# A 3x3 convolution on one core: two images on the partitions in place of two halves of one, inputs resident, and a different first and last stage

## The chip, the core and the metric

The kernel runs on one NeuronCore of a Trainium2 chip. The metric is the device time of one execution in microseconds (us). A second view is one profiled execution, whose span runs from the first to the last instruction.

## What is computed

A batch of 16 images of 64 channels, 64 by 64, is convolved with 128 filters of 64 x 3 x 3, with a border of zeros. A tenth of the weights is non-zero, but the kernels here treat them as dense.

```python
x:      (16, 64, 64, 64) float32
weight: (128, 64, 3, 3)  float32, about 90% zeros
x_pad = np.pad(x, ((0, 0), (0, 0), (1, 1), (1, 1)))
for b, co, ci, kh, kw:
    output[b, co] += weight[co, ci, kh, kw] * x_pad[b, ci, kh:kh+64, kw:kw+64]
output: (16, 128, 64, 64) float32
```

## The kernel before

For each of the nine taps (kh, kw), TensorE multiplies the tap's 64 x 128 weights by the input rows, shifted by the tap, and adds up in PSUM. One tap has only 64 input channels, so it fills half of the 128 rows of the array. The kernel therefore uses both halves at once: of each image, the upper 33 rows lie on partitions 0 to 63 and the lower 33 rows on partitions 64 to 127. One matmul for the upper half and one for the lower half stand next to each other in the program and run side by side. The 33rd row is read twice, since both halves need the rows at the seam.

A unit of work is 8 output rows of each half: two PSUM tiles (of 8, one bank each), nine pairs of matmuls of up to 512 columns (L175), then two copies from PSUM to the float32 output image in SBUF. An image has four units; the last unit of image 15 is split in two of 4 rows.

**Start.** The weights come in one transfer on SP's queue (L64), are cast to bf16 by VectorE in three pieces (L70), and are transposed on TensorE against an identity matrix (L84): nine taps, once for each half of the partitions, 18 small matmuls, copied out by ScalarE (L91). The identity is built on GpSimd (`make_identity`). Image 0 is loaded in four transfers, the first ten rows of each half first (L54 to L59). All loads of x are issued by GpSimd and cast float32 to bf16 on the way.

**Middle.** Images 1 to 14 are loaded in pairs into three buffers `xsg` (L107, L111), so from the fourth pair on a load waits until a buffer has been used up. Copies from PSUM alternate between ScalarE and VectorE (L186). Images 0, 1 and 12 leave in one transfer each (L202), images 2 to 11 in transfers of two images (L204), all on SP's queue.

**End.** Images 13, 14 and 15 are streamed: after each unit, both its blocks leave in one transfer, by turns on SP's queue (L197) and ScalarE's (L199).

The order of instructions on each engine is that of the program, as the tile framework schedules it; it sets waits where a buffer is reused.

Of the kernel before, what the change touches and what calls it, by code (L numbers as in the profile page):

```python
# [1 line left out]

# [6 lines left out]
FP32 = mybir.dt.float32  # L10
BF16 = mybir.dt.bfloat16


POS_ORDER = [(1, 1), (1, 0), (1, 2), (0, 0), (0, 1), (0, 2), (2, 0), (2, 1), (2, 2)]
CHUNK_ORDER = [1, 0, 2]


@with_exitstack
def kernel(
# [6 lines left out]
    nc = tc.nc  # L26

    B, C_IN, H, W = x.shape
    C_OUT, C_IN2, KH, KW = weight.shape
    assert (C_IN, H, W) == (64, 64, 64) and (C_OUT, KH, KW) == (128, 3, 3)  # L30

    HALF = H // 2
    XROWS = HALF + 1
    SPLIT = 10

    SINGLE_OUT = {0, 1, 12}
    PAIR_OUT_START = {2, 4, 6, 8, 10}
    STREAM_OUT = {13, 14, 15}
    UNITS_8 = [(r, 8) for r in range(0, HALF, 8)]
    STREAM_UNITS = {  # L40
        13: UNITS_8,
        14: UNITS_8,
        15: [(0, 8), (8, 8), (16, 8), (24, 4), (28, 4)],
    }

    const_pool = ctx.enter_context(tc.tile_pool(name="const", bufs=1))
    x0_pool = ctx.enter_context(tc.tile_pool(name="x0", bufs=2))
    xg_pool = ctx.enter_context(tc.tile_pool(name="xg", bufs=3))
    outs_pool = ctx.enter_context(tc.tile_pool(name="osb", bufs=3))
    outg_pool = ctx.enter_context(tc.tile_pool(name="osbg", bufs=2))  # L50
    psum_pool = ctx.enter_context(tc.tile_pool(name="psum", bufs=8, space=bass.MemoryType.PSUM))

    xs0 = x0_pool.tile([128, XROWS, W], BF16, name="xs0")
    nc.gpsimd.dma_start(out=xs0[0:64, 0:SPLIT], in_=x[0, :, 0:SPLIT, :])  # L54
    nc.gpsimd.dma_start(  # L55
        out=xs0[64:128, 0:SPLIT], in_=x[0, :, H - XROWS : H - XROWS + SPLIT, :]
    )
    nc.gpsimd.dma_start(out=xs0[0:64, SPLIT:XROWS], in_=x[0, :, SPLIT:XROWS, :])  # L58
    nc.gpsimd.dma_start(  # L59
        out=xs0[64:128, SPLIT:XROWS], in_=x[0, :, H - XROWS + SPLIT : H, :]  # L60
    )

    w_sb = const_pool.tile([C_OUT, C_IN * KH * KW], FP32)
    nc.sync.dma_start(out=w_sb, in_=weight.rearrange("o i kh kw -> o (i kh kw)"))  # L64
    w_sb3 = w_sb.rearrange("o (i k) -> o i k", k=KH * KW)

    w_bf = const_pool.tile([C_OUT, C_IN * KH * KW], BF16)
    w_bf3 = w_bf.rearrange("o (i k) -> o i k", k=KH * KW)
    for kh in CHUNK_ORDER:
        nc.vector.tensor_copy(  # L70
            out=w_bf3[:, :, kh * KW : (kh + 1) * KW],
            in_=w_sb3[:, :, kh * KW : (kh + 1) * KW],
        )

    ident = const_pool.tile([128, 128], BF16)
    make_identity(nc, ident)

    wT = const_pool.tile([128, KH * KW, C_OUT], BF16)
    for kh in CHUNK_ORDER:
        wps = psum_pool.tile([128, 4, 128], FP32, name="psum_t")  # L80
        for j in range(KW):
            sl = w_bf3[:, :, kh * KW + j]
            for half in range(2):
                nc.tensor.matmul(  # L84
                    wps[half * 64 : (half + 1) * 64, j, :],
                    sl,
                    ident,
                    start=True,
                    stop=True,
                )  # L90
        nc.scalar.copy(out=wT[:, kh * KW : kh * KW + KW, :], in_=wps[:, 0:KW, :])  # L91

    xs_group = None
    oimg_pair = None

    for b in range(B):
        if b == 0:
            xs = xs0
            xsel = ()
        elif b == B - 1:  # L100
            xs = x0_pool.tile([128, XROWS, W], BF16, name="xs15")
            nc.gpsimd.dma_start(out=xs[0:64], in_=x[b, :, 0:XROWS, :])  # L102
            nc.gpsimd.dma_start(out=xs[64:128], in_=x[b, :, H - XROWS : H, :])  # L103
            xsel = ()
        elif b % 2 == 1:
            xs_group = xg_pool.tile([128, 2, XROWS, W], BF16, name="xsg")
            nc.gpsimd.dma_start(  # L107
                out=xs_group[0:64].rearrange("i n r c -> i n (r c)"),
                in_=x[b : b + 2, :, 0:XROWS, :].rearrange("n i r c -> i n (r c)"),
            )  # L110
            nc.gpsimd.dma_start(  # L111
                out=xs_group[64:128].rearrange("i n r c -> i n (r c)"),
                in_=x[b : b + 2, :, H - XROWS : H, :].rearrange(
                    "n i r c -> i n (r c)"
                ),
            )
            xs = xs_group
            xsel = (0,)
        else:
            xs = xs_group  # L120
            xsel = (1,)

        if b in SINGLE_OUT or b in STREAM_OUT:
            oimg = outs_pool.tile([C_OUT, H, W], FP32, name="oimg")
        elif b in PAIR_OUT_START:
            oimg_pair = outg_pool.tile([C_OUT, 2, H, W], FP32, name="oimg2")
            oimg = oimg_pair[:, 0]
        else:
            oimg = oimg_pair[:, 1]

        streamed = b in STREAM_OUT
        if streamed:
            oimg_blk = oimg.rearrange("o (blk r) c -> o blk r c", blk=2)
            out_blk = out[b].rearrange("o (blk r) c -> o blk r c", blk=2)
            units = STREAM_UNITS[b]
        else:
            units = UNITS_8

        for ui, (ur0, rb) in enumerate(units):
            psums = []  # L140
            infos = []
            for half in range(2):
                r0 = half * HALF + ur0
                r1 = r0 + rb
                start_row = 0 if half == 0 else H - XROWS
                pbase = half * 64
                psum_t = psum_pool.tile([128, rb, W], FP32, name="psum_t")
                psums.append(psum_t)
                infos.append((r0, r1, start_row, pbase))

            for idx, (kh, kw) in enumerate(POS_ORDER):
                di, dj = kh - 1, kw - 1
                for half in range(2):
                    r0, r1, start_row, pbase = infos[half]
                    psum_t = psums[half]

                    i_lo = max(r0, -di)
                    i_hi = min(r1, H - di)
                    j_lo = max(0, -dj)
                    j_hi = min(W, W - dj)  # L160

                    rel_lo, rel_hi = i_lo - r0, i_hi - r0
                    xr_lo = i_lo + di - start_row
                    xr_hi = i_hi + di - start_row
                    xc_lo, xc_hi = j_lo + dj, j_hi + dj

                    idx_rhs = (slice(pbase, pbase + 64),) + xsel + (
                        slice(xr_lo, xr_hi),
                        slice(xc_lo, xc_hi),
                    )  # L170
                    rhs = xs[idx_rhs]
                    out_ap = psum_t[:, rel_lo:rel_hi, j_lo:j_hi]
                    lhsT = wT[pbase : pbase + 64, kh * KW + kw, :]

                    nc.tensor.matmul(  # L175
                        out_ap,
                        lhsT,
                        rhs,
                        start=(idx == 0),
                        stop=(idx == len(POS_ORDER) - 1),  # L180
                    )

            if not streamed:
                for half in range(2):
                    r0, r1, _, _ = infos[half]
                    nc.any.tensor_copy(out=oimg[:, r0:r1, :], in_=psums[half])  # L186
            else:
                nc.vector.tensor_copy(  # L188
                    out=oimg[:, infos[0][0] : infos[0][1], :], in_=psums[0]
                )  # L190
                nc.scalar.copy(  # L191
                    out=oimg[:, infos[1][0] : infos[1][1], :], in_=psums[1]
                )
                src = oimg_blk[:, :, ur0 : ur0 + rb, :]
                dst = out_blk[:, :, ur0 : ur0 + rb, :]
                if ui % 2 == 0:
                    nc.sync.dma_start(out=dst, in_=src)  # L197
                else:
                    nc.scalar.dma_start(out=dst, in_=src)  # L199

        if b in SINGLE_OUT:
            nc.sync.dma_start(out=out[b], in_=oimg)  # L202
        elif (b - 1) in PAIR_OUT_START:
            nc.sync.dma_start(  # L204
                out=out[b - 1 : b + 1].rearrange("n o h w -> o n (h w)"),
                in_=oimg_pair.rearrange("o n h w -> o n (h w)"),
            )


# [28 lines left out]
```

## Time and profile before

| what | us |
|---|---|
| median of 3 runs | 137.68 (137.21 to 138.09) |
| span of the profiled execution | 136.1 |
| TensorE busy, in 1188 matmuls | 126.7 |
| weight loads on TensorE, beside them | 77.1 |
| VectorE busy | 45.2 |
| ScalarE busy | 40.2 |
| first product (L175) starts | 5.92 |
| last copy from PSUM starts | 131.54 |

The profiled execution has no time of its own beside its span: what lies around the span is taken from the median, 137.68 - 136.1 = 1.5 us. The DMA engines moved 42.67 MB as they count it (a load that casts is counted by its bf16 bytes); at HBM it is 17.60 MB read and 33.55 MB written.

In the lines of the profile, a group reads: line, engine, operation, what it writes and reads, how often, then busy time and the mean of one in ns. PE is the matmul, PEld the weight load, DVE VectorE, ACT ScalarE, POOL GpSimd, SP SyncE; an engine's name with a q is its queue, here the issue of a DMA. The slices on the page are fortieths of the span.

### The profile page before, as it was taken

The numbers are of one execution on the slowest core, as the hardware profiler recorded it, in microseconds if no ns is written. First come the engines' busy times: TensorE is split into PE (matmuls) and PEld (weight loads), VectorE is DVE, ScalarE is ACT, GpSimd is POOL, SyncE is SP. The second block draws the span as 40 slices with busy tenths as digits, with TensorE's granted clock in tenths as the row PEclk, the third lists the DMA queues.
The fourth block names the chain that finished last, engine by engine and source line by source line (L and its number), as shares of the span: only waits on it lengthen the run. The fifth ranks groups of instructions, "written<-read, shape, count | busy, mean of one in ns | idle before, by whom it ended". The sixth has DMA issues, their size and how long they took to land.

```text
span 136.1 us, 2653 instructions
## 1 busy us (share of the span) xinstructions
PE 126.7 (93%) x1188; PEld 77.1 (57%) x1188; DVE 45.2 (33%) x68; ACT 40.2 (30%) x69; POOL 12.2 (9%) x26
## 2 busy tenths in 40 slices
PE   0699999999999999999999999999999999999960
PEld 0555666666565656665656655665656655656650
DVE  0203432344234432343234423443244333443240
ACT  3302332233323332233223332333233323332230
POOL 6950000003000110003000110000000000000000
PEclk9999999999999999999999999999999999999999
DMA  4999999999999999999999999999509999999884
GB/s 104 119 189 211 216 229 350 363 342 363 245 226 409 443 338 195 302 416 443 274 205 393 438 395 228 294 405 455 231 10 462 385 453 409 389 404 393 329 326 157
DMA packets 7980, 42.67 MB, mean 313 GB/s; under 512 B 673, under 2 KB 1313, under 8 KB 6305
## 3 DMA queue, kind: packets, MB, share of 16 engines
q1 hardware_dynamic: 3840, 30.97, 55.6%
q0 software_dynamic: 2496, 8.65, 33.4%
q10 hardware_dynamic: 1632, 2.88, 5.6%
q8 instruction: 9, 0.15, 0.4%
q14 instruction: 3, 0.02, 0.0%
HBM read 17.60 MB, written 33.55 MB: 376 GB/s over the span
## 4 chain that ended last, share of the span: by engine, by line
PE 92%; POOL 2%; issue 1%; ACT 1%; ACTq 0%; POOLq 0%
PE psum_t L175 91%; PE psum_t L84 1%; ACT oimg L191 1%; POOL xs L54 0%; ACTq L199 0%; POOL xs L55 0%; POOL xsg L107 0%; POOL xs L58 0%; POOL ident masks.py:199 0%; POOL ident masks.py:197 0%; POOL xs L59 0%; POOLq masks.py:199 0%; POOLq L222 0%
## 5 line engine op out<-in xcount | busy, mean ns | idle before, releaser
L175 PE MATMUL psum_t<-xsg,wT 64*128 64x512 bf16 (+2 forms) x1008 | 108.1, 374 | 0.0
L175 PEld LDWEIGHTS <-wT 64*128 64x128 bf16 x1170 | 75.8, 95 | 49.6 <-issue 1.9
L186 DVE COPY oimg<-psum_t 128x512 f32<-128x512 f32 x52 | 36.0, 692 | 68.6 <-PE psum_t L175 68.6
L186 ACT COPY oimg<-psum_t 128x512 f32<-128x512 f32 x52 | 30.5, 586 | 71.7 <-PE psum_t L175 71.7
L175 PE MATMUL psum_t<-xs,wT 64*128 64x504 bf16 (+5 forms) x162 | 18.0, 378 | 0.0
L188 DVE COPY oimg<-psum_t 128x512 f32<-128x512 f32 (+1 forms) x13 | 8.5, 650 | 14.3 <-PE psum_t L175 14.3
L191 ACT COPY oimg<-psum_t 128x512 f32<-128x512 f32 (+1 forms) x13 | 7.2, 554 | 16.0 <-PE psum_t L175 16.0
L107 POOL DMA_DIRECT2D xsg<-in_x_dram x7 | 4.2, 599 | 64.4 <-PE psum_t L175 64.4
L84 PE MATMUL psum_t<-ident,w_bf 128*64 128x128 bf16 x18 | 1.3, 321 | 4.7 <-POOL ident masks.py:199 4.7
L111 POOL DMA_DIRECT2D xsg<-in_x_dram x7 | 4.2, 607 | 0.0
L84 PEld LDWEIGHTS <-w_bf 128*64 128x64 bf16 x18 | 1.3, 208 | 4.5 <-DVE w_bf L70 4.1
L91 ACT CAST wT<-psum_t 128x384 bf16<-128x384 f32 x3 | 1.2, 487 | 3.3 <-PE psum_t L84 3.3
L70 DVE CAST w_bf<-w_sb 128x192 bf16<-128x192 f32 x3 | 0.8, 345 | 3.7 <-DMA w_sb<-in_weight_dram 3.7
L91 ACT ACT_TABLE_LOAD x1 | 1.3, 1283 | 0.7 <-PEq L222 0.7
L54 POOL DMA_DIRECT2D xs<-in_x_dram x1 | 0.7, 659 | 0.8 <-POOLq L222 0.8
L102 POOL DMA_DIRECT2D xs<-in_x_dram x1 | 0.5, 527 | 0.9 <-DMA xs<-in_x_dram 0.9
L103 POOL DMA_DIRECT2D xs<-in_x_dram x1 | 0.5, 522 | 0.4 <-DMA xs<-in_x_dram 0.4
L59 POOL DMA_DIRECT2D xs<-in_x_dram x1 | 0.6, 554 | 0.0
L55 POOL DMA_DIRECT2D xs<-in_x_dram x1 | 0.5, 542 | 0.0
L58 POOL DMA_DIRECT2D xs<-in_x_dram x1 | 0.5, 542 | 0.0
masks.py:199 POOL TENSOR_SCALAR_AFFINE_SELECT ident<-ident 128x128 bf16<-128x128 bf16 x1 | 0.4, 397 | 0.1
masks.py:197 POOL MEMSET ident<- 128x128 bf16 x1 | 0.3, 266 | 0.0
(4 smaller groups left out, 0.4 us busy)
## 6 DMA issues: line engine op xcount, KB each, us to landing
out_dram<-oimg SPq DMA_DIRECT2D x5, 4096.0 KB, 14.3
xsg<-in_x_dram POOLq DMA_DIRECT2D x14, 528.0 KB, 10.5
out_dram<-oimg SPq DMA_DIRECT2D x3, 2048.0 KB, 12.3
out_dram<-oimg SPq DMA_DIRECT2D x6, 512.0 KB, 7.0
out_dram<-oimg ACTq DMA_DIRECT2D x5, 512.0 KB, 6.8
xs<-in_x_dram POOLq DMA_DIRECT2D x2, 264.0 KB, 27.3
xs<-in_x_dram POOLq DMA_DIRECT2D x2, 184.0 KB, 6.0
w_sb<-in_weight_dram SPq DMA_DIRECT2D x1, 288.0 KB, 3.0
```

Source lines behind the costliest of these rows:

```text
L54: nc.gpsimd.dma_start(out=xs0[0:64, 0:SPLIT], in_=x[0, :, 0:SPLIT, :])
L55: nc.gpsimd.dma_start(out=xs0[64:128, 0:SPLIT], in_=x[0, :, H - XROWS : H - XROWS + SPLIT, :])
L59: nc.gpsimd.dma_start(out=xs0[64:128, SPLIT:XROWS], in_=x[0, :, H - XROWS + SPLIT : H, :])
L70: nc.vector.tensor_copy(out=w_bf3[:, :, kh * KW : (kh + 1) * KW], in_=w_sb3[:, :, kh * KW : (kh + 1) * KW],)
L84: nc.tensor.matmul(wps[half * 64 : (half + 1) * 64, j, :], sl, ident, start=True, stop=True,)
L91: nc.scalar.copy(out=wT[:, kh * KW : kh * KW + KW, :], in_=wps[:, 0:KW, :])
L107: nc.gpsimd.dma_start(out=xs_group[0:64].rearrange("i n r c -> i n (r c)"), in_=x[b : b + 2, :, 0:XROWS, :].rearrange("n i r c -> i n (r c)"),
L111: nc.gpsimd.dma_start(out=xs_group[64:128].rearrange("i n r c -> i n (r c)"), in_=x[b : b + 2, :, H - XROWS : H, :].rearrange("n i r c -> ...
L175: nc.tensor.matmul(out_ap, lhsT, rhs, start=(idx == 0), stop=(idx == len(POS_ORDER) - 1),)
L186: nc.any.tensor_copy(out=oimg[:, r0:r1, :], in_=psums[half])
L188: nc.vector.tensor_copy(out=oimg[:, infos[0][0] : infos[0][1], :], in_=psums[0])
L191: nc.scalar.copy(out=oimg[:, infos[1][0] : infos[1][1], :], in_=psums[1])
```

## The change

The kernel is rewritten around the same product. What it does:

- **Layout.** Two whole images lie on the partitions: image 2p on 0 to 63, image 2p + 1 on 64 to 127, in a tile of 128 x 64 x 64 bf16. A unit of work is the same 8 rows of both images. No row is read twice. The two PSUM tiles are copied by fixed engines, ScalarE for the first image and VectorE for the second.
- **Inputs.** All eight pairs have a tile of their own. Pair 0 comes in three pieces: rows 0 to 8 as float32 on ScalarE's queue (`x_head`), rows 9 to 25 and 26 to 63 by GpSimd with the cast. Pairs 1 to 7 are issued by GpSimd after the identity is built, one transfer each, with no buffer to wait for. ScalarE casts `x_head` into the tile of pair 0.
- **Start of TensorE.** Seven matmuls of 512 columns run on a tile of zeros, into a PSUM tile that nobody reads, ahead of the transposes.
- **Weights.** The cast to bf16 goes in six pieces and lays out, for each kh, the taps kw = 0, 1, 2, 0. A transpose takes two neighbouring taps at once, so that one matmul of 128 x 128 fills both halves of the partitions: nine in place of 18. The tap for the second image is read from a place shifted by one. Of the three groups, two are copied out by ScalarE and one by VectorE.
- **Order.** The order of instructions is that of the program (`manual_schedule`).
- **Outputs.** Seven output tiles of one image. Pairs 0 to 6: two transfers of 2 MB on SP's queue when the pair is done. Pair 7: rows 0 to 31 of both images after half of it, rows 32 to 47 after three quarters, then 8 rows of each image twice, one on SP's queue and one on ScalarE's.

The core of the new code:

```python
    xs = [x_pool.tile([128, H, W], BF16, name=f"x{p}") for p in range(NP)]
    nc.sync.dma_start(out=w_sb, in_=weight.rearrange("o i kh kw -> o (i kh kw)"))
    nc.scalar.dma_start(out=x_head, in_=pair(0)[:, 0:HEAD, :])               # HEAD = 9
    nc.gpsimd.dma_start(out=xs[0][:, HEAD:CUT, :], in_=pair(0)[:, HEAD:CUT, :])  # CUT = 26
    nc.gpsimd.dma_start(out=xs[0][:, CUT:H, :], in_=pair(0)[:, CUT:H, :])
    make_identity(nc, ident)
    for p in range(1, NP):
        nc.gpsimd.dma_start(out=xs[p], in_=pair(p))

    nc.vector.memset(idle_rhs, 0.0)
    for _ in range(7):
        nc.tensor.matmul(idle_ps, idle_rhs[:, 0:128], idle_rhs, start=True, stop=True)
    nc.scalar.copy(out=xs[0][:, 0:HEAD, :], in_=x_head)

    for g in (G1, G0, G2):
        for a, b in ((0, 3), (3, 4)):
            k = 3 * g + a % 3
            nc.vector.tensor_copy(out=w_bf4[:, g, a:b, :], in_=w_v[:, k : k + b - a, :])
    transposed(G1, nc.scalar.copy)       # 3 matmuls against ident, then the copy
    transposed(G0, nc.vector.tensor_copy)
    transposed(G2, nc.scalar.copy)

    for p in range(NP):
        o = [o_pool.tile([C_OUT, H, W], FP32, name="o") for _ in range(2)]   # 7 buffers
        last = p == NP - 1
        for blk in range(4):
            r0 = 16 * blk
            for r in (r0, r0 + 8):
                direct(p, o, r, 8)       # 9 pairs of matmuls, copy on ACT and on DVE
                if last and blk == 3:
                    nc.sync.dma_start(out=out[2 * p][:, r : r + 8, :], in_=o[0][:, r : r + 8, :])
                    nc.scalar.dma_start(
                        out=out[2 * p + 1][:, r : r + 8, :], in_=o[1][:, r : r + 8, :]
                    )
            if last and blk in (1, 2):
                a, b = (0, 32) if blk == 1 else (32, 48)
                for n in range(2):
                    nc.sync.dma_start(out=out[2 * p + n][:, a:b, :], in_=o[n][:, a:b, :])
        if not last:
            for n in range(2):
                nc.sync.dma_start(out=out[2 * p + n], in_=o[n])
```

## The prediction

> **What bounds the kernel now.** I read the page first (busy shares, slices, the chain), then the timeline of the first 14 us and the DMA queue's timeline, then groups by form in a cold and a warm window, and last the DMA share in windows near the end. The page:
>
> ```profile
> PE 126.7 (93%) x1188; PEld 77.1 (57%) x1188; DVE 45.2 (33%) x68; ACT 40.2 (30%) x69; POOL 12.2 (9%) x26
> ...
> DMA  4999999999999999999999999999509999999884
> GB/s 104 119 189 211 216 229 350 363 342 363 245 226 409 443 338 195 302 416 443 274 205 393 438 395 228 294 405 455 231 10 462 385 453 409 389 404 393 329 326 157
> ...
> PE 92%; POOL 2%; issue 1%; ACT 1%; ACTq 0%; POOLq 0%
> ```
>
> TensorE is busy for 93% and is 92% of the chain of waits. But the DMA engines are nearly full too, except in slices 29 and 30 (95 to 102 us). So there are two resources to follow, and the second has little room. The start, from the timeline:
>
> ```profile
> 0.74 0.40 SPq L64 DMA_DIRECT2D w_sb<-in_weight_dram  x1
> ...
> 3.72 0.77 DVE L70 CAST w_bf<-w_sb 128x192 bf16<-128x192 f32 x3 [3.72 <-DMA w_sb<-in_weight_dram]
> ...
> 4.69 1.30 PE L84 MATMUL psum_t<-ident,w_bf 128*64 128x128 bf16 x18 [4.69 <-POOL ident masks.py:199]
> ...
> 5.92 8.32 PE L175 MATMUL psum_t<-xs,wT 64*128 64x512 bf16 x57
> ...
> 8.73 0.22 PEld L175 LDWEIGHTS <-wT 64*128 64x128 bf16 x2 [0.21 <-issue]
> ...
> 9.15 0.22 PEld L175 LDWEIGHTS <-wT 64*128 64x128 bf16 x2 [0.21 <-issue]
> ...
> 9.58 4.39 PEld L175 LDWEIGHTS <-wT 64*128 64x128 bf16 x40 [0.21 <-issue]
> ```
>
> The weights land at 3.7, the identity is ready at 4.7, and the products start at S = 5.92. Until about 9.9 a pair of weight loads comes every 0.42 us (8.73, 9.15, 9.58); after that 40 loads take 4.39 us, 0.22 a pair. The matmuls themselves say the same, first the window 6.3 to 9.5, then 40 to 60:
>
> ```profile
> L175 PE MATMUL psum_t<-xs,wT 64*128 64x504 bf16 x9 | 3.3, 630 | 0.0
> ```
> ```profile
> L175 PE MATMUL psum_t<-xsg,wT 64*128 64x504 bf16 x117 | 20.2, 377 | 0.0
> ```
>
> The page's clock row shows full speed throughout, but 630 ns against 377 for one form is a slow array, about 0.5 of the later pace. From 5.92 to 9.9, some 9.5 pairs took 4.0 us where 9.5 x 0.216 = 2.1 would do: a cold loss C = 1.9 us. The output queue gives the steady pace and the end:
>
> ```profile
> 39.80 61.97 SPq L204 DMA_DIRECT2D out_dram<-oimg  x5
> ```
> ```profile
> 130.18 2.29 SPq L197 DMA_DIRECT2D out_dram<-oimg  x2
> ```
>
> Five issues, the last of which itself takes 0.37: (61.97 - 0.37) / 4 = 15.40 us for two images. Then 5.92 + 1.9 + 8 x 15.40 = 131.0 is the end of the products, 0.5 later the last result starts to be copied, the copy takes 0.37 and the last issue comes at about 131.94. It lands 3.2 later (256 KB, next fence) and the span ends 1.0 after that, 136.1. So today the end is TensorE plus a short tail. What the DMA engines can do (windows: length, busy time of each engine, clock, DMA share, GB/s; then three issues with KB and us to landing):
>
> ```profile
> 98.00:101.00 3.00, 3.00 (x32) 1.82 (x29) 1.06 (x2) 1.13 (x2) 0.00 (x0) 1.00 0.05 22
> 101.00:102.20 1.20, 1.20 (x16) 0.69 (x13) 0.32 (x1) 0.04 (x1) 0.00 (x0) 1.00 0.00 0
> 106.00:109.00 3.00, 3.00 (x32) 1.80 (x30) 1.36 (x2) 1.17 (x2) 0.00 (x0) 1.00 0.98 421
> 112.00:115.00 3.00, 3.00 (x30) 1.82 (x28) 1.38 (x2) 1.17 (x2) 0.00 (x0) 1.00 1.02 426
> 118.00:121.00 3.00, 3.00 (x31) 1.80 (x29) 1.15 (x2) 1.15 (x2) 0.00 (x0) 1.00 1.04 402
> ```
> ```profile
> out_dram<-oimg SPq DMA_DIRECT2D x1, 4096.0 KB, 11.9
> ...
> out_dram<-oimg SPq DMA_DIRECT2D x1, 256.0 KB, 3.2
> ```
>
> Full engines write 0.42 MB/us in large packets and 0.405 in the streamed 2 KB ones. A 4 MB output issued to idle engines (101.4) lands after 11.9 us: 4.19 / 0.42 = 10.0 plus 1.9 of start and completion.
>
> **The change part by part.** The sum is made against the profiled span of 136.1; the median of the runs is 137.68, so 1.5 us lie around it, and I add them at the end.
>
> *Steady products.* Still 9 pairs of matmuls for 8 rows of two tiles, the same 64x128 weight loads and 512 columns: 15.40 us per two images, 123.2 in all. Edge rows (441 and 448 columns, 350 ns against 377) were spread over the two halves before and meet in one pair now; the saving is in the 15.40 already, since the half that ran ahead at the top is caught up at the bottom. The split last unit goes: -0.05, taken as 0. Copies are pinned, one ACT (586 ns) and one DVE (692 ns) per 1.94 us: hidden with over 1.2 us of room each.
>
> *Inputs.* POOL issues 9 casts instead of 18, all without waiting for a buffer (64.4 us of its waits on products go). They cost nothing as long as a pair arrives before its turn, every 15.4 us: 2 MB read at the 0.42 of a full engine is 5 us alone, 10 if shared evenly with outputs. Output tiles come round after 7 images: image 7 needs tile 0, issued near 21.5 and needed near 52; it may take 30 us where the longest issue took 15. Nothing.
>
> *Rows 9 to 63 of the first pair.* Rows 9 to 25 (272 KB of bf16) are needed one block after S, near 7.8. Nearest rows: two of 80 KB landed in 3.6 us and two of 184 KB in 6.0, from issues between 1.2 and 2.9. So 5 to 7.5; between 0 and 0.7 late, and I take 0, since they are now first in the queue.
>
> *Weights landing, T.* The raw head (288 KB on ACT's queue) leaves with the weights (288 KB on SP's, 0.74). Weights alone landed at 3.7. Between no delay, and the whole transfer ahead of it at the 236 GB/s the engines reach from 2 to 3 us (1.25): I take 0.7, since two queues served in turn end together near the sum's end. T = 4.4, bounds 3.7 to 4.95.
>
> *From T to the products.* Six casts on DVE in place of three (345 ns each, 0.21 apart by 0.77 for three); three are a third of the size, estimate 1.07 for all. Nine transposes in place of 18, and TensorE takes all before a product: T + 1.25. ACT casts the head first (estimate 0.65, from 586 ns for 512 columns), then the first weight group (487 ns) once its transposes are out at T + 0.9: T + 1.45, the later. The identity, behind two POOL issues and not five, is ready before T. S = 4.4 + 1.45 = 5.85, bounds 5.15 to 6.4. Against 5.92 that is next to nothing.
>
> *Seven idle matmuls.* A memset, then 7 x 0.43 = 3.0 us from about 1.1 to 4.1, before anything they could delay. In the trace the array sped up at 9.9, 5.2 us after its first work at 4.69; the same 5.2 from 1.1 gives 6.3, a loss of (6.3 - 5.85) / 2 = 0.2. If the gap from 4.1 to T + 0.4 starts the count again, C stays at 1.9. Below 0 it can't be. I take 0.2, as the array then works in most of 1.1 to 6.3, against a gap of 0.7. Here a rule speaks against the change. The Trainium skill, "TensorE: Matmul & The Clock Gate", Part 1, says that the clock doubles after a window of about 3.4 us of sustained work, in windows that run freely; 3.0 us of idle work don't fill one, and by that rule alone C would stay near 1.9 and the sum would be 141.1 instead of 139.4. No row here shows the window's threshold.
>
> *The last outputs.* Here the change costs. Before, images 12 to 15 left singly, the last three in 512 KB pieces from 111 us on. Now image pair 6 leaves whole, when its last row is copied, and of pair 7 half leaves at its middle, a quarter at three quarters, the rest in two steps. The issue of pair 6 comes at S + C + 7 x 15.40 + 0.45 + 0.59 = S + C + 108.85. From there 8.39 MB must go, whatever TensorE does. The engines are idle just before: pair 5's 11.9 us end inside the 15.4 between issues, as at 98 to 102 above (inputs and six pairs, 42 MB, need 100 us of 0.42 by then). Pair 6: 11.9. Then with no gap, as each next piece is issued (+116.6, +120.5, +122.4, +124.3) before the one ahead is done: 2.10 / 0.42 = 5.0, 1.05 / 0.42 = 2.5, 1.05 / 0.405 = 2.6. Last landing S + C + 131.85 - 1.0 = S + C + 130.85, and the end 1.0 later.
>
> *Sum.* S + C = 5.85 + 0.2 = 6.05, against 7.82 before: 1.8 us won at the start. End 6.05 + 131.85 = 137.9 against 136.1: the tail takes back 3.5. With the 1.5 around it, 139.4.
>
> **Rivals.** *The tail is hidden (faster).* If only TensorE set the end: products S + C + 123.2, 0.45 and 0.69 for the copy, 3.2 to landing, 1.0: S + C + 128.5 = 134.6, so 136.1. That needs 8.39 MB in 3.3 us less than 20.1, 0.50 MB/us; below that rate the queue decides. Against it: 421 and 426 GB/s at a DMA share of 1; only one slice of the page shows more than 0.455 (462, just after the idle one). *The idle matmuls don't do what they are said to:* C = 1.9, 141.1. For it: only 3.0 us of work, then a gap; against it: 5.2 us of partly sparse work were enough before. *Early start:* the head costs the weights nothing and C = 0: S + C = 5.15, 138.5. For it: the DMA share between 2 and 3 us was 0.80, so there is a little room. *Rows 9 to 25 or the weights come later than thought,* POOL's casting transfers taking turns with both: 1.0 more, 140.4. For it: the GB/s row is at 119 in the second slice.
>
> **How the numbers follow.** Chances: the forecast 0.58, cold array 0.20, early start 0.12, late rows 0.06, hidden tail 0.04. Prediction 139.4. The forecast's own range is 138.6 to 140.3, S between its bounds, and the rate 0.42 +- 0.01 (0.5 us over 20). The range 138.2 to 141.2 takes in the early start and the cold array and leaves out the hidden tail and sums of two mishaps. A measurement here can tell about 1%, 1.4 us: faster below 136.3, only the hidden tail, 0.04. Same up to 139.1: the early start and the lower fifth of the forecast, 0.12 + 0.13 = 0.25. Slower 0.71.
>
> **What would show it.** Weights landing near 4.4 and the first product near 5.9; matmuls of 377 ns from the first or second pair on; issues 15.4 apart; DMA idle before pair 6's issue near 114.9 and full from 116 to the end; the last issue about 6.5 us before its landing, not 3.2. I am wrong if the last landing follows its issue by 3 us (the queue had kept up), if early matmuls take 630 ns, or if a product waits for an input or an output tile.

## The result and the profile after

The changed kernel takes 141.51 us (median of 4 runs, 140.85 to 142.61) against 137.87 for the kernel before (137.21 to 138.09): a ratio of 1.029 with an interval of 1.023 to 1.036. The prediction was 139.4 with a range of 138.2 to 141.2. Its sign was right and the size was not: about 3.6 us lost where 1.7 were forecast. The four runs stand in two places, 140.85 and 140.87, and 142.15 and 142.61; the profiled one is of the second. The profiled execution took 142.15, with a span of 140.4; the span forecast was 137.9.

A ratio here leaves out executions that lie over 1.5% above the fastest of the same kernel; the medians keep them, so the two can differ.

The page of the changed kernel first:

```profile
PE 129.0 (92%) x1168; PEld 57.1 (41%) x1168; DVE 46.7 (33%) x72; ACT 40.4 (29%) x68; POOL 5.6 (4%) x15
...
DMA  4999999999999999999999954993099707999992
GB/s 109 240 223 215 217 203 224 187 303 327 299 336 334 317 301 320 360 430 420 420 439 434 430 238 177 420 448 154 2 448 432 317 5 299 383 439 399 405 392 79
...
PE 90%; DMA 3%; DVE 1%; issue 0%
```

The chain still says TensorE, because the instruction that ended last on an engine is a copy of a product at 131.9. The span goes on to 140.4. Read only the chain, and the last 8.4 us are not there. They are in the waits of SP's queue, whose last wait is for outputs to land. After, then before:

```profile
SPq L168 <- DMA out_dram<-o: 6.7, 5, 2.0
```
```profile
SPq L233 <- DMA out_dram<-oimg: 2.3, 3, 1.1
```

The slices show the shape: slices 29 and 33 are idle, because pairs 4 and 5 have left and the next is not done; then the engines are full to the end. In numbers, from when pair 6 is issued (window, length, busy PE, PEld, DVE, ACT and POOL, clock, DMA share, GB/s):

```profile
115.00:118.00 3.00, 3.00 (x34) 1.41 (x30) 0.91 (x2) 0.85 (x2) 0.00 (x0) 1.00 0.39 164
118.00:121.00 3.00, 3.00 (x32) 1.32 (x30) 1.17 (x2) 0.91 (x2) 0.00 (x0) 1.00 0.93 393
...
130.00:133.00 3.00, 1.20 (x12) 0.38 (x8) 0.79 (x2) 0.59 (x1) 0.00 (x0) 1.00 1.00 408
133.00:136.00 3.00, 0.00 (x0) 0.00 (x0) 0.00 (x0) 0.00 (x0) 0.00 (x0) 0.87 1.02 393
136.00:139.00 3.00, 0.00 (x0) 0.00 (x0) 0.00 (x0) 0.00 (x0) 0.00 (x0) 0.50 0.55 203
```

The products end in the window of 130 to 133. For 3 us more the DMA engines are full with no compute at all, and then half full. The last pieces (KB, us to landing) against 3.2 us for the last one before:

```profile
out_dram<-o SPq DMA_DIRECT2D x2, 256.0 KB, 8.2
out_dram<-o ACTq DMA_DIRECT2D x2, 256.0 KB, 6.3
```

The start, from the timeline of the first 16 us:

```profile
0.74 0.40 ACTq L51 DMA_DIRECT2D x_head<-in_x_dram  x1
0.74 0.38 SPq L50 DMA_DIRECT2D w_sb<-in_weight_dram  x1
...
1.19 3.17 PE L64 MATMUL ps<-idle_rhs 128*128 128x512 bf16 x7 [1.19 <-DVE idle_rhs L61]
...
4.74 1.67 DVE L88 CAST w_bf<-w_sb 128x192 bf16<-128x192 f32 x6 [3.60 <-DMA w_sb<-in_weight_dram]
4.90 0.67 ACT L66 CAST x<-x_head 128x576 bf16<-128x576 f32 x1 [2.45 <-DMA x_head<-in_x_dram]
...
5.83 0.48 ACT L83 CAST wT<-ps 128x384 bf16<-128x384 f32 x1 [0.26 <-PE ps L82]
6.34 0.24 PEld L82 LDWEIGHTS <-w_bf 128*128 128x128 bf16 x3 [0.29 <-DVE w_bf L88]
...
6.78 9.56 PE L108 MATMUL ps<-x,wT 64*128 64x512 bf16 x78
...
8.41 0.15 PEld L108 LDWEIGHTS <-wT 64*128 64x128 bf16 x2 [0.22 <-issue]
8.79 7.28 PEld L108 LDWEIGHTS <-wT 64*128 64x128 bf16 x68 [0.22 <-issue]
```

The weights land at 4.72 (3.70 before), six casts follow for 1.67 us, TensorE waits for them between groups of transposes, and the first product starts at 6.78 (5.92 before). The pairs come slowly until 8.8 and at 0.21 us after that. The start won nothing: S + C, the start and the cold loss together, is 6.78 + 1.06 = 7.84 here, against 7.82 before. (C is the time from the first to the last product, 130.84 - 6.78, less 123.0 at the steady pace.)

So the whole loss of this execution lies at its end. The last copy from PSUM starts at 131.26, where it started at 131.54 before; the products are not late, and the output queue runs on.

### The profile page after: what moved, and what is told of

It reads as the page before. It is cut to its first block, busy times and chain, and to the rows that moved or that the text cites. A ratio compares the mean times of both kernels' runs of the same rounds, so it can differ in the third digit from the quotient of the medians.

```text
span 140.4 us, 2591 instructions
## 1 busy us (share of the span) xinstructions
PE 129.0 (92%) x1168; PEld 57.1 (41%) x1168; DVE 46.7 (33%) x72; ACT 40.4 (29%) x68; POOL 5.6 (4%) x15
## 4 chain that ended last, share of the span: by engine, by line
PE 90%; DMA 3%; DVE 1%; issue 0%
PE ps L108 89%; DMA w_sb<-in_weight_dram 3%; PE ps L82 1%; DVE o L122 0%; DVE w_bf L88 0%
## 5 line engine op out<-in xcount | busy, mean ns | idle before, releaser
L108 PE MATMUL ps<-x,wT 64*128 64x504 bf16 (+3 forms) x1152 | 124.4, 377 | 0.0
L108 PEld LDWEIGHTS <-wT 64*128 64x128 bf16 x1152 | 55.5, 95 | 68.7 <-issue 1.5
L122 DVE COPY o<-ps 128x512 f32<-128x512 f32 x64 | 44.3, 692 | 80.8 <-PE ps L108 80.8
L121 ACT COPY o<-ps 128x512 f32<-128x512 f32 x64 | 37.5, 586 | 86.9 <-PE ps L108 86.9
L64 PE MATMUL ps<-idle_rhs 128*128 128x512 bf16 x7 | 3.2, 630 | 1.2 <-DVE idle_rhs L61 1.2
L57 POOL DMA_DIRECT2D x<-in_x_dram x7 | 3.7, 553 | 0.2 <-issue 0.2
L88 DVE CAST w_bf<-w_sb 128x192 bf16<-128x192 f32 (+1 forms) x6 | 1.7, 347 | 3.6 <-DMA w_sb<-in_weight_dram 3.6
L82 PE MATMUL ps<-ident,w_bf 128*128 128x128 bf16 x9 | 1.5, 306 | 1.0 <-DVE w_bf L88 0.9
L64 PEld LDWEIGHTS <-idle_rhs 128*128 128x128 bf16 x7 | 0.9, 139 | 2.6 <-issue 1.4
L83 ACT CAST wT<-ps 128x384 bf16<-128x384 f32 x2 | 1.0, 479 | 0.8 <-PE ps L82 0.8
L52 POOL DMA_DIRECT2D x<-in_x_dram x1 | 0.7, 664 | 0.8 <-POOLq L157 0.8
L53 POOL DMA_DIRECT2D x<-in_x_dram x1 | 0.5, 537 | 0.0
```

What stands on the lines that cost most here:

```text
L52: nc.gpsimd.dma_start(out=xs[0][:, HEAD:CUT, :], in_=pair(0)[:, HEAD:CUT, :])
L53: nc.gpsimd.dma_start(out=xs[0][:, CUT:H, :], in_=pair(0)[:, CUT:H, :])
L57: nc.gpsimd.dma_start(out=xs[p], in_=pair(p))
L64: nc.tensor.matmul(idle_ps, idle_rhs[:, 0:128], idle_rhs, start=True, stop=True)
L82: nc.tensor.matmul(wps[:, j, :], src, ident, start=True, stop=True)
L83: copy(out=wT[:, g], in_=wps[:, 0:3, :])
```

## The experiments

Two theories stood against each other for the size of the loss. *Queue:* 8.39 MB are left when pair 6 is done, and full DMA engines set the end. *Pieces or start:* the way in which pair 7 is cut, or the late start, is the loss. For the start there were two more: what holds the weights, and what decides when the array becomes fast. Each kernel below was timed beside the kernel before on the same chip (medians of the kernel before 137.25 to 137.52); ratios are to it.

### Half of pair 6 leaves earlier (p6half)

```diff
+            if p == NP - 2 and blk == 1:
+                for n in range(2):
+                    nc.sync.dma_start(out=out[2 * p + n][:, 0:32, :], in_=o[n][:, 0:32, :])
...
+            a = 32 if p == NP - 2 else 0
...
-                nc.sync.dma_start(out=out[2 * p + n], in_=o[n])
+                nc.sync.dma_start(out=out[2 * p + n][:, a:H, :], in_=o[n][:, a:H, :])
```

> The changed kernel, but rows 0 to 31 of both images of pair 6 leave at its middle instead of its end: 2.1 MB fewer are left when pair 6 is done. In the changed kernel's trace the last transfer lands 7.6 us after its issue, where an unqueued one of that size took 3.2. Queue theory (the output queue sets the end): 2.1 MB / 0.42 = 5.0 us less backlog, more than the 4.4 in excess, so the last landing follows its issue by about 3.2 to 3.8 and the time falls by 3.8 to 4.4 from 141.5, to 137.1 to 137.7, with the products as late as before. Rival, the last pieces are slow by themselves (their number, two queues, small rows): a fall of 0.5 at most. Rival, the late start is the whole loss: no fall.

Measured: 139.2, ratio 1.007 (1.003 to 1.012) against 1.029: about 3.0 us won. That is well over the 0.5 that a slow set of last pieces would give, and below the 3.8 expected. The reason for the rest is in its own profile:

```profile
out_dram<-o SPq DMA_DIRECT2D x2, 256.0 KB, 4.5
out_dram<-o ACTq DMA_DIRECT2D x2, 256.0 KB, 4.4
```

The last pieces still land 4.4 us after their issue, not 3.2: the queue is shorter but not empty.

One caution: this profile and that of halves below are executions in which the array was fast early (S + C = 6.41 in both, against 7.84 in the changed kernel's). Of the 4.1 us between the spans, 140.4 and 136.2, the start gives 1.4 and not the edit. The times are not misled by this: the runs of p6half lie at 137.4 to 138.1 and at 139.2 to 139.8, the changed kernel's at 140.9 and at 142.2 to 142.6, and from place to place the fall is about 3 us.

### All of pair 7 in small pieces, pair 6 whole (p7stream)

```diff
-                if last and blk == 3:
+                if last:
...
-            if last and blk in (1, 2):
-                a, b = (0, 32) if blk == 1 else (32, 48)
-                for n in range(2):
-                    nc.sync.dma_start(out=out[2 * p + n][:, a:b, :], in_=o[n][:, a:b, :])
```

> The changed kernel, but pair 7 leaves 8 rows at a time from its first block on, one image on SP's queue and one on ScalarE's; pair 6 still leaves whole. Queue theory: the engines are busy with pair 6 until half of pair 7 is done, so the same 8.39 MB run through the same full engines: between -0.5 and +0.7 (2 KB rows instead of 8 and 4 KB run at 0.405 instead of 0.42 MB/us, 0.2 us on 3.1 MB). Rival, the staging of pair 7 (a half, then a quarter) is what costs: a fall of 2 to 4.

Measured: 142.92, ratio 1.034 (1.026 to 1.042). Against 1.029 that is 0.5% or 0.7 us more, at the edge of what was expected and within both intervals; a fall of 2 to 4 is excluded. In its profile the last landing comes 23.47 us after pair 6's issue, 0.5 more than in the changed kernel's. Issuing the last pair's rows sooner buys nothing while the pair before it fills the engines. The queue theory stands, and the staging of pair 7 is not the cost.

### Every output in halves (halves)

```diff
-            if last and blk in (1, 2):
-                a, b = (0, 32) if blk == 1 else (32, 48)
-                for n in range(2):
-                    nc.sync.dma_start(out=out[2 * p + n][:, a:b, :], in_=o[n][:, a:b, :])
-        if not last:
-            for n in range(2):
-                nc.sync.dma_start(out=out[2 * p + n], in_=o[n])
+            if last and blk < 3:
+                for n in range(2):
+                    nc.sync.dma_start(out=out[2 * p + n][:, r0 : r0 + 16, :], in_=o[n][:, r0 : r0 + 16, :])
+            elif not last and blk in (1, 3):
+                a = r0 - 16
+                for n in range(2):
+                    nc.sync.dma_start(out=out[2 * p + n][:, a : a + 32, :], in_=o[n][:, a : a + 32, :])
```

> The changed kernel with all outputs in smaller parts: pairs 0 to 6 leave in halves of 32 rows, pair 7 in 16 rows and at the end 8 and 8. Start and products untouched. With pair 6 halved alone the last landing was still 4.4 us after its issue. Theory: now it is 3.2 to 3.7, so 0.7 to 1.2 less than with pair 6 halved alone, and 3.5 to 4.5 below the changed kernel. Rival, the rest of that kernel's excess is the late start alone: no less than with pair 6 halved.

Measured: 137.97, ratio 1.001 (0.997 to 1.006): 2.8% or 3.8 us below the changed kernel, level with the kernel before. The queue's last wait and the last pieces:

```profile
SPq L168 <- DMA out_dram<-o: 2.1, 4, 0.6
```
```profile
out_dram<-o SPq DMA_DIRECT2D x2, 256.0 KB, 2.7
out_dram<-o ACTq DMA_DIRECT2D x2, 256.0 KB, 3.1
```

6.7 us of waiting have become 2.1. Its runs lie at 136.5 and at 137.7 to 138.6, in either place some 4 us below the changed kernel's. This one edit, which touches nothing but when outputs leave, undoes the loss against the kernel before.

### The same tail in the kernel before (beforetail)

```diff
-    SINGLE_OUT = {0, 1, 12}
-    PAIR_OUT_START = {2, 4, 6, 8, 10}
-    STREAM_OUT = {13, 14, 15}
+    SINGLE_OUT = {0, 1}
+    PAIR_OUT_START = {2, 4, 6, 8, 10, 12}
+    STREAM_OUT = {14, 15}
```

> The kernel before, but images 12 and 13 leave as one transfer of 4 MB when 13 is done, instead of one of 2 MB and a streamed image; 14 and 15 are streamed as they were. Start and products untouched. Queue theory: 8.39 MB are left when image 13 is done, near 116.8; 1.9 + 8.39 / 0.415 = 22.1 later the last lands, 138.9, and the span ends at 139.9, +3.8 on 136.1. Rival, the kernel before is bound by TensorE at its end and hides this: +0.5 at most.

Measured: 143.39, ratio 1.040 (1.034 to 1.046): 5.5 us more. The direction and the mechanism are as expected, with the rest of that kernel untouched:

```profile
SPq L233 <- DMA out_dram<-oimg: 7.3, 2, 6.4
```

The size is 1.7 above the 3.8 expected. In its profiled execution (span 141.7), 0.2 come from a later issue (117.02) and 1.3 from the queue itself: 23.4 us from the issue to the last landing and not 22.1; another 0.3 lie between that landing and the end. What is known of the 1.3 stands in the hardware section.

### The head behind the weights (wfirst)

```diff
-    nc.scalar.dma_start(out=x_head, in_=pair(0)[:, 0:HEAD, :])
+    nc.sync.dma_start(out=x_head, in_=pair(0)[:, 0:HEAD, :])
```

> The changed kernel, but the raw head x_head is issued on SP's queue behind the weights instead of on ScalarE's beside them. In the changed kernel's trace the weights land at 4.72, 1.0 later than in the kernel before (3.70). Theory that the two transfers take turns on the same engines: the weights land at 3.7 to 3.9 again, the head at about 4.7, products start near 5.9 instead of 6.8, the whole time falls by 0.6 to 1.0 (the cold loss can take part of it back). Rival, something else delays the weights (GpSimd's loads, which start at 2.9): they land at 4.5 or later and nothing changes.

Measured: 140.26, ratio 1.021 (1.015 to 1.027), 0.8% or 1.2 us below the changed kernel. The two intervals overlap, so the time alone leaves it open; the trace does not. The casts start at 3.7 and the products a microsecond earlier:

```profile
3.73 1.68 DVE L88 CAST w_bf<-w_sb 128x192 bf16<-128x192 f32 x6 [2.60 <-DMA w_sb<-in_weight_dram]
...
5.06 0.47 ACT L83 CAST wT<-ps 128x384 bf16<-128x384 f32 x1
...
5.78 2.59 PE L108 MATMUL ps<-x,wT 64*128 64x512 bf16 x18
```

The weights land at 3.71, as in the kernel before, and the head at 4.46, which is earlier than when it was issued beside them on a queue of its own (4.88). best1 below has the same edit: weights at 3.75, head at 4.76. In the seven traces with the head beside the weights, these land between 4.41 and 4.88. So the second transfer delayed the weights by 0.7 to 1.2, and gained nothing for itself. The Trainium skill ("DMA: Bandwidth & Descriptors", Issuing engines are not separate DMA queues) has transfers from all issuers interleave on the same engines, so that issuing from several saves only issue time, and these runs agree. From the issue of pair 6 to the last landing it is 114.95 to 137.93, 22.99 us: the tail is the same and starts 1.5 earlier, 1.0 by the start and 0.5 by a smaller cold loss (C = 0.57).

### A later third group of transposes (lazy)

```diff
-    transposed(G2, nc.scalar.copy)
+    late = {1: (G2, nc.scalar.copy)}
...
+            if i in late:
+                transposed(*late.pop(i))
```

> The changed kernel, but the three transposes of the third weight group come behind the first pair of products instead of ahead of it. In the changed kernel's trace TensorE waits for VectorE's six casts (4.74 to 6.41), does the last transposes at 6.35 to 6.6 and starts the products at 6.78, while the first group's weights were ready at 6.31. Theory that the casts and not ScalarE hold the first product: it starts near 6.35, 0.4 earlier, and the time falls by 0.3 to 0.5 unless the slow array takes it. Rival, ScalarE's copy of the first group is the last to end: no earlier than 6.7 and no gain.

Measured: 142.36, ratio 1.034 (1.028 to 1.040): no gain. But the first product did start as the theory has it:

```profile
4.52 1.67 DVE L88 CAST w_bf<-w_sb 128x192 bf16<-128x192 f32 x6 [3.39 <-DMA w_sb<-in_weight_dram]
...
6.14 0.61 PE L110 MATMUL ps<-x,wT 64*128 64x512 bf16 x2
...
7.12 3.14 PE L110 MATMUL ps<-x,wT 64*128 64x504 bf16 x20
...
8.70 0.14 PEld L110 LDWEIGHTS <-wT 64*128 64x128 bf16 x2 [0.23 <-issue]
9.01 0.96 PEld L110 LDWEIGHTS <-wT 64*128 64x128 bf16 x10 [0.17 <-issue]
```

S is 1.64 after the landing (6.14 - 4.50) instead of 2.06, so the casts did hold it. The second pair then waits for the moved transposes, and the array becomes fast at 8.95, as in the changed kernel (8.93). With C = 1.67, S + C is 7.81 against 7.84: nothing. An earlier start under a slow array, whose end does not move, gains half of itself at most, and the moved transposes took that.

### No idle work (noidle), and idle work without a gap (dense)

noidle:

```diff
-    nc.vector.memset(idle_rhs, 0.0)
...
-    for _ in range(7):
-        nc.tensor.matmul(idle_ps, idle_rhs[:, 0:128], idle_rhs, start=True, stop=True)
```

dense:

```diff
-    for _ in range(7):
+    for _ in range(9):
...
+    def filler():
+        nc.tensor.matmul(idle_ps[:, 0:256], idle_rhs[:, 0:128], idle_rhs[:, 0:256], start=True, stop=True)
...
     transposed(G1, nc.scalar.copy)
+    filler()
     transposed(G0, nc.vector.tensor_copy)
+    filler()
```

> The changed kernel without the seven matmuls on zeros and their tile. In the changed kernel the first products still ran at 0.42 us a pair and the fast pace came at 8.9, a loss of 1.05 us after the start at 6.78. Theory that the idle work brings the fast clock forward but not far enough: without it the loss grows to about 1.9, as in the kernel before (window 1.0 to 2.8): +0.9. Rival, the count starts again at the gap before the transposes, and the idle work does nothing: 0 +- 0.3. Start of the products unchanged at 6.8 in both.

Measured: 142.78, ratio 1.037 (1.029 to 1.044). That is 0.7% above the changed kernel, in the direction of the first theory, but the intervals overlap: the times don't settle it. The profile speaks for the rival:

```profile
6.94 5.31 PE L103 MATMUL ps<-x,wT 64*128 64x512 bf16 x38
...
9.29 2.69 PEld L103 LDWEIGHTS <-wT 64*128 64x128 bf16 x26 [0.19 <-issue]
```

Its products start at 6.94, the pairs are fast from 9.3, and the loss C is 1.14, not 1.9. In this pair of profiled executions the seven idle matmuls brought the fast pace forward by 0.3 us (9.24 to 8.93 in the record of the granted clock) and lowered C by less than 0.1. Other executions can differ; the hardware section has more on this.

> The changed kernel with nine idle matmuls instead of seven, and one of 256 columns between the groups of transposes, so that the array has work nearly without a gap from 1.2 us to the first product. Theory that the gap from 4.1 to 5.3 is what lets some executions stay slow (fast pace at 8.9 in the changed kernel's profile, at 5.3 in that of the kernel with pair 6 halved): every execution reaches the fast pace before 7, the loss is below 0.3, the runs lie closer together, and the median falls by 0.6 to 1.0 against the changed kernel. Rival, it depends on nothing that the kernel does before the products: no change.

Measured: 140.99, ratio 1.027 (1.022 to 1.032), 0.3 to 0.5 us below the changed kernel, which the intervals don't separate; the fall of 0.6 to 1.0 that was expected did not come. What does show is the spread: four runs from 140.82 to 141.21, where the changed kernel's four lie from 140.85 to 142.61. In its profile the second pair of products is already fast (window 6.6 to 9.0), where the changed kernel's early ones are not (6.7 to 8.7):

```profile
L113 PE MATMUL ps<-x,wT 64*128 64x504 bf16 x10 | 1.6, 377 | 0.0
```
```profile
L108 PE MATMUL ps<-x,wT 64*128 64x504 bf16 x4 | 1.1, 630 | 0.0
```

So work without a gap can make the array fast by 7. With the changed kernel's own start it is fast from the first product in two traces (p6half and halves, C = 0.02) and late in two (the changed kernel and p7stream). Its runs at 140.85 and 140.87 lie where an execution with S + C = 6.41 would, 142.15 - 1.43 = 140.7 by estimate, but no trace shows them.

### The idle work alone, in the kernel before (beforeidle)

```diff
+    idle_rhs = const_pool.tile([128, 512], BF16, name="idle_rhs")
+    nc.vector.memset(idle_rhs, 0.0)
+    idle_ps = psum_pool.tile([128, 8, W], FP32, name="psum_t")
+    for _ in range(8):
+        nc.tensor.matmul(idle_ps, idle_rhs[:, 0:128], idle_rhs, start=True, stop=True)
```

> The kernel before with eight matmuls on zeros ahead of its transposes (a tile of zeros set by VectorE, 8 x 0.43 = 3.4 us from 1.2 to 4.6), nothing else. Theory that the idle work moves the fast pace forward where there is no gap behind it: the loss of 1.9 us after the first product falls to 0 to 0.6, the time by 1.2 to 1.9, to 135.6 to 136.3. Rival, the output stream of the last three images has no room and takes the gain back (its pieces land 3.2 after their issue only because the products are late): a fall of 0.5 or less.

Measured: 136.0, ratio 0.991 (0.988 to 0.994): 0.9% or 1.3 us faster than the kernel before, in all nine runs between 135.79 and 136.66. The products start at 5.92 as before, and are fast from the first pair (window 5.8 to 8.0):

```profile
L181 PE MATMUL psum_t<-xs,wT 64*128 64x504 bf16 x10 | 1.8, 377 | 0.0
```

Here the idle work ends at 4.8, the transposes start at 4.72, and no gap lies between. Its output stream keeps up: the last piece lands 3.18 after its issue, as before.

### All three repairs (best1)

```diff
-    nc.scalar.dma_start(out=x_head, in_=pair(0)[:, 0:HEAD, :])
+    nc.sync.dma_start(out=x_head, in_=pair(0)[:, 0:HEAD, :])
...
     transposed(G1, nc.scalar.copy)
+    filler()                       # as in dense
     transposed(G0, nc.vector.tensor_copy)
+    filler()
...
+                    nc.sync.dma_start(out=out[2 * p + n][:, a : a + 32, :], in_=o[n][:, a : a + 32, :])
```

The outputs leave as in halves; the idle matmuls ahead of the transposes stay seven.

> All three repairs: outputs in halves and smaller, head behind the weights, and a 256-column idle matmul between the groups of transposes (seven before them, as the weights are expected near 3.8). If start, clock and tail are the whole loss, S + C is 5.9 to 6.2 and TensorE sets the end: S + C + 128.5 = 134.4 to 134.7, and 1.7 around it: 136.1 to 136.4, 0.8 to 1.2% faster than the kernel before. If a fourth cause is left, not below the kernel before (137.5 to 137.9).

Measured: 136.35, ratio 0.992 (0.989 to 0.995). It is faster than both kernels and inside the time expected of start, clock and tail together, so no fourth cause of a size that shows is left. (S + C is 6.40 in its profile, 0.2 above the expected bounds.) Two of its twelve runs are at 139.3 and 140.0, and why is not known. The idle work alone in the kernel before does as well, with none of the rest.

## Why the prediction was wrong in size

Its sum was S + C + 131.85 = 137.9 of span, with S + C = 6.05; the profile has 140.4. Two steps of the start failed, the way from the weights to the first product and the idle matmuls, and the tail's mechanism was right but its size too small. Point by point:

- **Steady products, inputs, output tiles: right.** Issues of whole pairs stand 15.40 apart (24.04 to 116.44 in six steps), no product waits for an input and no copy for an output tile. Rows 9 to 25 landed at 6.07, in time. (The first pair's issue, put near 21.5, comes at 22.5 by the prediction's own terms and came at 24.04; with some 28 us to spare it cost nothing.)
- **The last outputs: right mechanism, 1.0 too short.** The engines were idle before pair 6 was issued and full after. The issue came at 116.44, within 0.25 of S + C + 108.85. From there to the last landing it took 22.98 and not 22.0; five kernels with this tail have 22.97 to 22.99. From 118 to 136 the engines moved 406 GB/s on average, a little under the 417 that the sum comes to (8.39 MB in 20.1 us). Then they are full to 137.3, and for the last 2 us one of them runs on alone (see the hardware section).
- **Weights landing: in the bounds, 0.3 late.** 4.72 against 4.4. The head's transfer cost 1.0 here and 0.7 to 1.2 over seven traces; 0.7 was taken.
- **From the landing to the products: failed, 0.6 too short.** It was given 1.45, with no bounds of its own, and took 2.06; so S, at 6.78, left its bounds of 5.15 to 6.4. The six casts took 1.67, where 1.07 was an estimate from three that overlapped: a large one took 0.49 and a small one 0.20, not the 0.345 and a third of it; TensorE takes all nine transposes before a product, and the last three wait for the last cast. lazy shows that this order held the start.
- **Seven idle matmuls: failed, 0.86 too cheap in this execution.** C was taken as 0.2 and was 1.06; early matmuls took 630 ns, which the prediction named as a sign of being wrong. The step that failed is the carrying over of "5.2 us after the first work" from one trace: by it the array would be fast at 6.3, and the record of the granted clock has 8.93. Among five traces with this start it is 4.29 to 9.52, so no fixed delay holds. The rival with a cold array was kept apart at 1.9; what came lies between, and differs from run to run.
- **Around the span: 0.3 too short.** 1.5 was a median less the span of another execution. In every timed run here the time is 1.7 to 1.9 longer than the run's own span.

0.3 + 0.6 + 0.86 + 0.7 (tail, less the earlier issue) come to the 2.5 of span that were missing. The rival that the tail would be hidden is excluded by p6half, halves and beforetail. The rival with the cold array, at 141.1, comes near the median of 141.51, but by luck: its S, its C and its tail are not those that were measured. What the sum got wrong is that it credited the start with 1.8 us, and in the profiled execution the start gave back none of it.

## What to carry to other kernels

When an output leaves only when a large part is done, count the bytes that are left at each issue against the rate of full DMA engines until the end: 8.39 MB at 0.42 MB/us is 20 us, whatever the compute does, and the chain of engine work does not show it; the last wait of the issuing queue does. Leave the first load that everything waits for alone on the queues. And before a whole start is rewritten, try the one piece of it that the trace supports: matmuls on zeros until the real ones begin, without a gap, were worth 0.9% by themselves in the kernel before.

## What the runs showed of the hardware

- **When the array becomes fast varies with the same start.** Five kernels share the seven idle matmuls from 1.19 to 4.36 and the gap after them. By the trace's record of the granted clock the full pace began at 4.29 (halves), 5.31 (p6half), 8.93 (the changed kernel), 8.95 (lazy) and 9.52 (p7stream). Without a gap it was 7.01 (dense), 6.93 (wfirst, whose transposes start as the idle work ends), 6.92 (best1) and 5.27 (beforeidle).
- **The traces point to a grid of 3.41 us.** The stretch of full clock lasts 126.29 us in ten of the twelve traces and 129.71 in halves and p6half: 37 and 38 steps of 3.413. Going back one step from the moment when the full pace began, matmuls filled that step to 80% or more in all twelve (p6half 80%, halves 91%, the others 98% or more). They filled the step before it to 79% at most (lazy 79%, beforetail 75%, p7stream 74%, the changed kernel 73%, dense 70%). By this reading, what decides is how much work falls between two lines of the grid, and where an execution lies on it is chance. No run set that on purpose, and the limit near 80% is only read from these twelve traces. The Trainium skill ("TensorE: Matmul & The Clock Gate", Part 1) has windows of about 3.4 us that run freely, and this scatter fits that. But halves got there after 3.1 us of work, before a full window's length had passed.
- **One of sixteen completions comes late in a full queue.** Each output reports sixteen completions. In the changed kernel the second image of pair 6 has fifteen by 127.84 and the last at 129.80; the last piece has fifteen by 138.07 and one at 139.42. beforetail has lags of 0.6 to 1.9. The end of the changed kernel shows it in the rate, in slices of 0.285 us from 129 on:

```profile
GB/s 287 431 460 460 431 431 402 402 402 374 316 403 431 446 417 331 431 431 366 438 367 359 402 374 381 395 381 381 417 273 29 22 29 22 29 7 0 0 0 0
```

After 137.5 some 25 GB/s are left, about a sixteenth of the full rate. Without the late completions the last landing would be at 138.24, 21.8 us after pair 6's issue, where 22.0 was forecast; by this reckoning they are the 1.0 us that the tail ran over. A transfer of instructions (16 KB, 0.96 us) ran beside it from 127.8, but whether it is the cause was not tried.
